# Two heads on the 128 partitions in place of one: softmax times V with 64 KB loads, 4 KB stores and products over the values of two heads

## The chip, the cores and the metric

One core of a Trainium2 chip runs the whole program. The metric is device time in microseconds (us), the median of several executions; smaller is better.

## The reference

```python
# scores [8, 12, 1024, 1024] f32, v [8, 12, 1024, 64] f32: 96 heads
scores_max = np.max(scores, axis=-1, keepdims=True)
attn = np.exp(scores - scores_max)
attn = attn / (np.sum(attn, axis=-1, keepdims=True) + 1e-8)
return np.matmul(attn, v).astype(np.float32)      # [8, 12, 1024, 64]
```

The scores are 4 MB per head, 403 MB in all, and each is used once. That is why the loads matter so much.

## The kernel before

One head at a time stands on the 128 partitions, with 8 query rows in each (`R = 8`). Its scores come as one 4 MB transfer, in which each partition receives one run of 32 KB. Four such tiles are in flight (`AHEAD = 4`), and the load of head n+4 is queued when head n has been read. ScalarE takes the exponential of two rows per partition and writes float16. TensorE transposes eight 128x128 blocks, VectorE copies them to SBUF, and TensorE multiplies them with the values and a column of ones, whose product is the sum of the row. VectorE divides, four rows at a time.

```python
    R = SQ // P          # 8
    M = D + 1            # 65
    EB = 2; G = 4; LAG = 2; NV = 3
    AHEAD = 4
    sc_bh = scores.rearrange("b h (p r) j -> (b h) p r j", p=P)
    # ... (cut: views of v and out, pools)
    s_pool = ctx.enter_context(tc.tile_pool(name="spool", bufs=AHEAD))
    # ... (cut)
    def finish(u):
        # ... (cut)
        for c in range(C):
            nc.tensor.matmul(out=psO[:, g, :], lhsT=pt[:, c * P : (c + 1) * P],
                             rhs=st["vones"][:, c, :], start=(c == 0), stop=(c == C - 1))
        if g == G - 1:
            # ... (cut: reciprocal of the sums)
            nc.vector.tensor_tensor(out=st["out_sb"][:, r - G + 1 : r + 1, :],
                in0=psO[:, :, 0:D], in1=recip[:].to_broadcast([P, G, D]), op=mybir.AluOpType.mult)
        if r == R - 1:
            queue(nc.sync.dma_start(out=out_bh[n], in_=st["out_sb"][:]))
    def load(n):
        v_sb = v_pool.tile([P, C, D], FP32, tag="v_sb", name="v_sb")
        queue(nc.sync.dma_start(out=v_sb[:], in_=v_bh[n]))
        s_nat = s_pool.tile([P, R, SK], FP32, tag="s_nat", name="s_nat")
        step = EB if n == BH - 1 else R          # the last head in four pieces
        for r in range(0, R, step):
            queue(nc.sync.dma_start(out=s_nat[:, r : r + step, :], in_=sc_bh[n, :, r : r + step, :]))
    # ... (cut)
        for r in range(R):
            if r % EB == 0:
                p_nat = p_pool.tile([P, EB, SK], FP16, tag="p_nat", name="p_nat")
                nc.scalar.activation(out=p_nat[:], in_=s_nat[:, r : r + EB, :], func=EXP)
            # ... (cut: eight transposes into psT, one copy to pt)
            if r == R - 1 and n + AHEAD < BH:
                load(n + AHEAD)
            # ... (cut: finish() two rows later)
```

All transfers are issued by one queue, in program order.

The softmax here doesn't subtract the row's maximum and nothing guards it: scores larger than these inputs give would overflow.

Of the kernel before, what the change touches and what calls it, by code (L numbers as in the profile page):

```python
# [1 line left out]

# [5 lines left out]

FP32 = mybir.dt.float32
FP16 = mybir.dt.float16  # L10
EXP = mybir.ActivationFunctionType.Exp


@with_exitstack
def kernel(
    ctx: ExitStack,
    tc: tile.TileContext,
    scores: bass.AP,
    v: bass.AP,
    out: bass.AP,  # L20
):
    nc = tc.nc
    P = 128

    B, H, SQ, SK = scores.shape
    Bv, Hv, SKv, D = v.shape
    assert (B, H, SK) == (Bv, Hv, SKv)
    BH = B * H
    assert SQ % P == 0 and SK % P == 0
    R = SQ // P  # L30
    C = SK // P
    M = D + 1
    EB = 2
    G = 4
    LAG = 2
    NV = 3
    AHEAD = 4



    sc_bh = scores.rearrange("b h (p r) j -> (b h) p r j", p=P)
    v_bh = v.rearrange("b h (p c) d -> (b h) p c d", p=P)
    out_bh = out.rearrange("b h (p r) d -> (b h) p r d", p=P)

    const_pool = ctx.enter_context(tc.tile_pool(name="const", bufs=1))
    s_pool = ctx.enter_context(tc.tile_pool(name="spool", bufs=AHEAD))
    p_pool = ctx.enter_context(tc.tile_pool(name="ppool", bufs=6))
    v_pool = ctx.enter_context(tc.tile_pool(name="vpool", bufs=AHEAD))
    pt_pool = ctx.enter_context(tc.tile_pool(name="ptpool", bufs=5))
    ob_pool = ctx.enter_context(tc.tile_pool(name="obpool", bufs=3))  # L50
    rc_pool = ctx.enter_context(tc.tile_pool(name="rcpool", bufs=4))
    psT_pool = ctx.enter_context(tc.tile_pool(name="psTp", bufs=5, space=bass.MemoryType.PSUM))
    psO_pool = ctx.enter_context(tc.tile_pool(name="psOp", bufs=3, space=bass.MemoryType.PSUM))

    ident32 = const_pool.tile([P, P], FP32, name="ident32")
    make_identity(nc, ident32)
    ident16 = const_pool.tile([P, P], FP16, name="ident16")
    nc.vector.tensor_copy(out=ident16[:], in_=ident32[:])  # L58


    vones_bufs = []
    for k in range(NV):
        vo = const_pool.tile([P, C, M], FP16, name=f"vones{k}")
        nc.vector.memset(vo[:, :, D : D + 1], 1.0)  # L64
        vones_bufs.append(vo)

    pending = []

    def finish(u):

        n, r, pt, st = u
        g = r % G
        if g == 0:
            st["psO"] = psO_pool.tile([P, G, M], FP32, tag="psO", name="psO")
        psO = st["psO"]
        for c in range(C):
            nc.tensor.matmul(  # L77
                out=psO[:, g, :],
                lhsT=pt[:, c * P : (c + 1) * P],
                rhs=st["vones"][:, c, :],  # L80
                start=(c == 0),
                stop=(c == C - 1),
            )
        if g == G - 1:
            if r == G - 1:
                st["out_sb"] = ob_pool.tile([P, R, D], FP32, tag="out_sb", name="out_sb")
            recip = rc_pool.tile([P, G, 1], FP32, tag="recip", name="recip")
            nc.vector.reciprocal(out=recip[:], in_=psO[:, :, D : D + 1])  # L88
            nc.vector.tensor_tensor(  # L89
                out=st["out_sb"][:, r - G + 1 : r + 1, :],  # L90
                in0=psO[:, :, 0:D],
                in1=recip[:].to_broadcast([P, G, D]),
                op=mybir.AluOpType.mult,
            )
        if r == R - 1:
            queue(nc.sync.dma_start(out=out_bh[n], in_=st["out_sb"][:]))  # L96

    queued = []

    def queue(dma):  # L100

        if queued:
            tc.add_manual_dep(
                dma.ins,
                queued[-1].ins.name,
                mybir.DependencyInfo(mybir.DependencyClass.NoSync, mybir.DependencyReason.DATA),
                reason="queue order",
            )
        queued.append(dma)

    loaded = {}

    def load(n):
        v_sb = v_pool.tile([P, C, D], FP32, tag="v_sb", name="v_sb")
        queue(nc.sync.dma_start(out=v_sb[:], in_=v_bh[n]))  # L115
        s_nat = s_pool.tile([P, R, SK], FP32, tag="s_nat", name="s_nat")
        step = EB if n == BH - 1 else R
        for r in range(0, R, step):
            queue(
                nc.sync.dma_start(out=s_nat[:, r : r + step, :], in_=sc_bh[n, :, r : r + step, :])  # L120
            )
        loaded[n] = (s_nat, v_sb)

    for n in range(min(AHEAD, BH)):
        load(n)

    for n in range(BH):
        s_nat, v_sb = loaded.pop(n)
        vones = vones_bufs[n % NV]
        nc.gpsimd.tensor_copy(out=vones[:, :, 0:D], in_=v_sb[:])  # L130
        st = dict(vones=vones)

        for r in range(R):
            if r % EB == 0:
                p_nat = p_pool.tile([P, EB, SK], FP16, tag="p_nat", name="p_nat")
                nc.scalar.activation(out=p_nat[:], in_=s_nat[:, r : r + EB, :], func=EXP)  # L136
            p_row = p_nat[:, r % EB, :].rearrange("p (q c) -> p c q", c=C)
            psT = psT_pool.tile([P, SK], FP16, tag="psT", name="psT")
            for c in range(C):
                nc.tensor.transpose(  # L140
                    out=psT[:, c * P : (c + 1) * P],
                    in_=p_row[:, c, :],
                    identity=ident16[:],
                )
            pt = pt_pool.tile([P, SK], FP16, tag="pt", name="pt")
            nc.vector.tensor_copy(out=pt[:], in_=psT[:])  # L146
            if r == R - 1 and n + AHEAD < BH:
                load(n + AHEAD)
            pending.append((n, r, pt, st))
            if len(pending) > LAG:  # L150
                finish(pending.pop(0))
    while pending:
        finish(pending.pop(0))


# [1 line left out]
_INS = ['scores', 'v']  # L157
_OUTS = [((8, 12, 1024, 64), 'float32')]


# [23 lines left out]
```

## Time and profile before

| | before |
|---|---|
| median of 3 executions | 1090.04 us (1089.73 to 1090.33) |
| span of the profiled one | 1088.4 us |
| DMA slices at 9 tenths | 39 of 40 |
| bytes moved | 454.77 MB, 418 GB/s on average |
| busiest compute engine | PE, 72% |
| head 93 landed / last scores landed / end | 1054.3 / 1077.1 / 1088.4 us |

### The profile page before, as it was taken

How to read it: one execution, taken by the hardware profiler on the slowest of the kernel's cores; microseconds unless marked ns; L12 is line 12 of the kernel's file. 1: busy time of each engine (PE TensorE's matmuls, PEld its weight loads, DVE VectorE, ACT ScalarE, POOL GpSimd, SP SyncE). 2: the span in 40 equal slices, each digit the busy share in tenths (PEclk: the TensorE clock that was granted, in tenths of full speed). 3: DMA queues.
4: the chain of work that ended last, by engine and by line, in shares of the span. 5: the costliest groups of instructions: out<-in, count | busy, mean ns of one | idle time of the engine just before them, and what ended most of it. 6: DMA issues, size and time to landing. Idle time of an engine off the chain costs nothing.

```text
span 1088.4 us, 27687 instructions
## 1 busy us (share of the span) xinstructions
PE 782.8 (72%) x12288; PEld 743.7 (68%) x12288; DVE 628.2 (58%) x1156; ACT 704.0 (65%) x385; POOL 60.1 (6%) x102
## 2 busy tenths in 40 slices
PE   3767777676777767677776767777676777767676
PEld 3667667676766767677676767677676767767676
DVE  2556556565555655556565655655565565556555
ACT  4667576666757666665766666575665757566675
POOL 0000000000000000000000000000000000000000
PEclk9888878778787877878888887878888787787888
DMA  9999999999999999999999999999999999999994
GB/s 396 423 430 425 423 423 427 427 426 428 427 422 423 424 431 427 422 426 424 431 425 429 425 426 424 425 429 428 424 423 430 424 426 427 428 420 428 426 398 160
DMA packets 42024, 454.77 MB, mean 418 GB/s; under 512 B 4656, under 2 KB 4656, under 8 KB 29232
## 3 DMA queue, kind: packets, MB, share of 16 engines
q1 hardware_dynamic: 41904, 453.00, 98.5%
q8 instruction: 96, 1.57, 0.6%
q14 instruction: 24, 0.20, 0.0%
HBM read 427.82 MB, written 25.17 MB: 416 GB/s over the span
## 4 chain that ended last, share of the span: by engine, by line
DMA 96%; DVE 1%; PE 1%; issue 0%; SPq 0%; ACT 0%; DVEq 0%; ACTq 0%
DMA out_dram<-out_sb 69%; DMA s_nat<-in_scores_dram 18%; DMA v_sb<-in_v_dram 9%; DVE out_sb L89 1%; PE psT L140 1%; PE psO L77 0%; SPq L120 0%; ACT p_nat L136 0%; DVE pt L146 0%; SPq L115 0%; DVE recip L88 0%; DVEq L89 0%; SPq L96 0%; ACTq L136 0%
## 5 line engine op out<-in xcount | busy, mean ns | idle before, releaser
L136 ACT ACTIVATE p_nat<-s_nat 128x2048 f16<-128x2048 f32 x384 | 702.8, 1901 | 375.8 <-DMA s_nat<-in_scores_dram 364.7
L140 PE MATMUL psT<-ident,p_nat 128*128 128x128 f16 x6144 | 621.6, 264 | 274.5 <-ACT p_nat L136 273.5
L140 PEld LDWEIGHTS <-p_nat 128*128 128x128 f16 x6144 | 524.9, 155 | 301.5 <-ACT p_nat L136 295.2
L146 DVE COPY pt<-psT 128x1024 f16<-128x1024 f16 x768 | 529.0, 691 | 307.2 <-PE psT L140 285.4
L77 PE MATMUL psO<-vones,pt 128*128 128x65 f16 x6144 | 343.0, 204 | 27.3 <-DVE pt L146 26.3
L77 PEld LDWEIGHTS <-pt 128*128 128x128 f16 x6144 | 295.4, 107 | 39.2 <-DVE pt L146 38.3
L89 DVE TENSOR_TENSOR out_sb<-psO,recip 128x256 f32<-128x256 f32 x192 | 73.6, 420 | 98.7 <-DMA out_dram<-out_sb 98.6
L130 POOL CAST vones<-v_sb 128x512 f16<-128x512 f32 x96 | 59.4, 619 | 1007.3 <-DMA v_sb<-in_v_dram 995.5
L88 DVE RECIPROCAL recip<-psO 128x4 f32<-128x4 f32 x192 | 34.1, 178 | 49.9 <-PE psO L77 49.9
L136 ACT ACT_TABLE_LOAD x1 | 1.3, 1283 | 0.7 <-PEq L168 0.7
L64 DVE MEMSET vones<- 128x8 f16 x3 | 0.1, 65 | 0.8 <-PEq L168 0.8
L58 DVE CAST ident<-ident 128x128 f16<-128x128 f32 x1 | 0.2, 227 | 0.4 <-POOL ident masks.py:199 0.4
masks.py:199 POOL TENSOR_SCALAR_AFFINE_SELECT ident<-ident 128x128 f32<-128x128 f32 x1 | 0.3, 294 | 0.1
masks.py:197 POOL MEMSET ident<- 128x128 f32 x1 | 0.2, 205 | 0.3 <-POOLq L168 0.3
L168 POOL MEMSET const-float32-0.0<- 128x1 f32 x1 | 0.1, 99 | 0.2 <-issue 0.2
L168 POOL MEMSET const-bfloat16-1.0<- 128x1 bf16 x1 | 0.1, 102 | 0.0
L168 POOL MEMSET const-uint8-127<- 128x1 uint8 x1 | 0.1, 102 | 0.0
L168 POOL MEMSET const-float32-1.0<- 128x1 f32 x1 | 0.1, 99 | 0.0
## 6 DMA issues: line engine op xcount, KB each, us to landing
s_nat<-in_scores_dram SPq DMA_DIRECT2D x95, 4096.0 KB, 32.5
v_sb<-in_v_dram SPq DMA_DIRECT2D x96, 256.0 KB, 23.5
out_dram<-out_sb SPq DMA_DIRECT2D x96, 256.0 KB, 32.4
s_nat<-in_scores_dram SPq DMA_DIRECT2D x4, 1024.0 KB, 23.8
```

What stands on the lines that cost most here:

```text
L58: nc.vector.tensor_copy(out=ident16[:], in_=ident32[:])
L64: nc.vector.memset(vo[:, :, D : D + 1], 1.0)
L77: nc.tensor.matmul(out=psO[:, g, :], lhsT=pt[:, c * P : (c + 1) * P], rhs=st["vones"][:, c, :], start=(c == 0), stop=(c == C - 1),)
L88: nc.vector.reciprocal(out=recip[:], in_=psO[:, :, D : D + 1])
L89: nc.vector.tensor_tensor(out=st["out_sb"][:, r - G + 1 : r + 1, :], in0=psO[:, :, 0:D], in1=recip[:].to_broadcast([P, G, D]), op=mybir.Al ...
L130: nc.gpsimd.tensor_copy(out=vones[:, :, 0:D], in_=v_sb[:])
L136: nc.scalar.activation(out=p_nat[:], in_=s_nat[:, r : r + EB, :], func=EXP)
L140: nc.tensor.transpose(out=psT[:, c * P : (c + 1) * P], in_=p_row[:, c, :], identity=ident16[:],)
L146: nc.vector.tensor_copy(out=pt[:], in_=psT[:])
L168: nc = _bacc.Bacc("TRN2", target_bir_lowering=False, num_devices=1)
```

## The change

The intent: let two heads share the partitions, 64 partitions each with 16 query rows, so that scores come as runs of 64 KB and the output leaves as runs of 4 KB. The partitions then belong to two heads, so a product takes the values of both heads at once (129 columns: 64 values, the ones, 64 values) and each half of the partitions keeps its own half. The tiles double, so two of them fit (`AHEAD = 2`).

```diff
-    R = SQ // P
-    M = D + 1
+    HALF = P // 2
+    NP = BH // 2
+    R = SQ // HALF          # 16
+    W = 2 * D + 1           # 129
-    AHEAD = 4
+    AHEAD = 2
-    sc_bh = scores.rearrange("b h (p r) j -> (b h) p r j", p=P)
+    sc = scores.rearrange("b h i j -> (b h i) j").rearrange("(k p r) j -> k p r j", p=P, r=R)
 ... (cut: v and out likewise; psT buffers 5 to 4, psO buffers 3 to 2)
-        step = EB if n == BH - 1 else R
-        for r in range(0, R, step):
+        cuts = [0, R]
+        if k == 0:
+            cuts = list(range(0, R + 1, 4))
+        if k == NP - 1:
+            cuts = list(range(0, R - 1, EB)) + [R - 1, R]
+        for a, b in zip(cuts, cuts[1:]):
+            queue(nc.sync.dma_start(out=s_nat[:, a:b, :], in_=sc[k, :, a:b, :]))
 ... (cut)
-                out=psO[:, g, :],
+                out=psO[:, g, 0:W],
 ... (cut)
-            nc.vector.tensor_tensor(... 128 partitions ...)
+            for h in range(2):
+                rows = slice(h * HALF, (h + 1) * HALF)
+                nc.vector.tensor_tensor(
+                    out=st["out_sb"][rows, r - G + 1 : r + 1, :],
+                    in0=psO[rows, :, h * (D + 1) : h * (D + 1) + D],
+                    in1=recip[rows].to_broadcast([HALF, G, D]),
 ... (cut)
-            if r == R - 1 and n + AHEAD < BH:
-                load(n + AHEAD)
+            if r == R - 1 and k + AHEAD < NP:
+                load(k + AHEAD)
```

The exponential of the very last two rows is also cut in two.

More of the change, by code (lines that the diff above doesn't have):

```diff
@@ L28 @@
     BH = B * H
-    assert SQ % P == 0 and SK % P == 0
-    R = SQ // P
+    HALF = P // 2
+    assert SQ % P == 0 and SK % P == 0 and BH % 2 == 0
+    NP = BH // 2
+    R = SQ // HALF
     C = SK // P
-    M = D + 1
+    W = 2 * D + 1
     EB = 2
@@ L36 @@
     NV = 3
-    AHEAD = 4
-    sc_bh = scores.rearrange("b h (p r) j -> (b h) p r j", p=P)
-    v_bh = v.rearrange("b h (p c) d -> (b h) p c d", p=P)
-    out_bh = out.rearrange("b h (p r) d -> (b h) p r d", p=P)
+    AHEAD = 2
+    sc = scores.rearrange("b h i j -> (b h i) j").rearrange("(k p r) j -> k p r j", p=P, r=R)
+    ov = out.rearrange("b h i d -> (b h i) d").rearrange("(k p r) d -> k p r d", p=P, r=R)
+    vv = v.rearrange("b h j d -> (b h) j d").rearrange("(k a) (p c) d -> k p a c d", a=2, p=P)
     const_pool = ctx.enter_context(tc.tile_pool(name="const", bufs=1))
@@ L51 @@
     rc_pool = ctx.enter_context(tc.tile_pool(name="rcpool", bufs=4))
-    psT_pool = ctx.enter_context(tc.tile_pool(name="psTp", bufs=5, space=bass.MemoryType.PSUM))
-    psO_pool = ctx.enter_context(tc.tile_pool(name="psOp", bufs=3, space=bass.MemoryType.PSUM))
+    psT_pool = ctx.enter_context(tc.tile_pool(name="psTp", bufs=4, space=bass.MemoryType.PSUM))
+    psO_pool = ctx.enter_context(tc.tile_pool(name="psOp", bufs=2, space=bass.MemoryType.PSUM))
     ident32 = const_pool.tile([P, P], FP32, name="ident32")
@@ L62 @@
     for k in range(NV):
-        vo = const_pool.tile([P, C, M], FP16, name=f"vones{k}")
+        vo = const_pool.tile([P, C, W], FP16, name=f"vones{k}")
         nc.vector.memset(vo[:, :, D : D + 1], 1.0)
@@ L67 @@
     pending = []
-    def finish(u):
-        n, r, pt, st = u
-        g = r % G
-        if g == 0:
-            st["psO"] = psO_pool.tile([P, G, M], FP32, tag="psO", name="psO")
-        psO = st["psO"]
-        for c in range(C):
-            nc.tensor.matmul(
-                out=psO[:, g, :],
-                lhsT=pt[:, c * P : (c + 1) * P],
-                rhs=st["vones"][:, c, :],
-                start=(c == 0),
-                stop=(c == C - 1),
-            )
-        if g == G - 1:
-            if r == G - 1:
-                st["out_sb"] = ob_pool.tile([P, R, D], FP32, tag="out_sb", name="out_sb")
-            recip = rc_pool.tile([P, G, 1], FP32, tag="recip", name="recip")
-            nc.vector.reciprocal(out=recip[:], in_=psO[:, :, D : D + 1])
-            nc.vector.tensor_tensor(
-                out=st["out_sb"][:, r - G + 1 : r + 1, :],
-                in0=psO[:, :, 0:D],
-                in1=recip[:].to_broadcast([P, G, D]),
-                op=mybir.AluOpType.mult,
-            )
-        if r == R - 1:
-            queue(nc.sync.dma_start(out=out_bh[n], in_=st["out_sb"][:]))
     queued = []
@@ L111, with load @@
     loaded = {}
-    def load(n):
-        v_sb = v_pool.tile([P, C, D], FP32, tag="v_sb", name="v_sb")
-        queue(nc.sync.dma_start(out=v_sb[:], in_=v_bh[n]))
+    def load(k):
+        v_sb = v_pool.tile([P, 2, C, D], FP32, tag="v_sb", name="v_sb")
+        queue(nc.sync.dma_start(out=v_sb[:], in_=vv[k]))
         s_nat = s_pool.tile([P, R, SK], FP32, tag="s_nat", name="s_nat")
-        step = EB if n == BH - 1 else R
-        for r in range(0, R, step):
-            queue(
-                nc.sync.dma_start(out=s_nat[:, r : r + step, :], in_=sc_bh[n, :, r : r + step, :])
-            )
-        loaded[n] = (s_nat, v_sb)
@@ L124 @@
-    for n in range(min(AHEAD, BH)):
-        load(n)
-    for n in range(BH):
-        s_nat, v_sb = loaded.pop(n)
-        vones = vones_bufs[n % NV]
-        nc.gpsimd.tensor_copy(out=vones[:, :, 0:D], in_=v_sb[:])
+        cuts = [0, R]
[5 more added lines that the diff above has]
+            queue(nc.sync.dma_start(out=s_nat[:, a:b, :], in_=sc[k, :, a:b, :]))
@@ new lines, in load, with finish @@
+        loaded[k] = (s_nat, v_sb)
+    def finish(u):
+        k, r, pt, st = u
+        g = r % G
+        if g == 0:
+            st["psO"] = psO_pool.tile([P, G, 256], FP32, tag="psO", name="psO")
+        psO = st["psO"]
+        for c in range(C):
+            nc.tensor.matmul(
+                out=psO[:, g, 0:W],
+                lhsT=pt[:, c * P : (c + 1) * P],
+                rhs=st["vones"][:, c, :],
+                start=(c == 0),
+                stop=(c == C - 1),
+            )
+        if g == G - 1:
+            if r == G - 1:
+                st["out_sb"] = ob_pool.tile([P, R, D], FP32, tag="out_sb", name="out_sb")
+            recip = rc_pool.tile([P, G, 1], FP32, tag="recip", name="recip")
+            nc.vector.reciprocal(out=recip[:], in_=psO[:, :, D : D + 1])
+            for h in range(2):
[4 more added lines that the diff above has]
+                    in1=recip[rows].to_broadcast([HALF, G, D]),
+                    op=mybir.AluOpType.mult,
+                )
+        if r == R - 1:
+            queue(nc.sync.dma_start(out=ov[k], in_=st["out_sb"][:]))
@@ L131 @@
+    for k in range(min(AHEAD, NP)):
+        load(k)
+    for k in range(NP):
+        s_nat, v_sb = loaded.pop(k)
+        vones = vones_bufs[k % NV]
+        for h in range(2):
+            nc.gpsimd.tensor_copy(
+                out=vones[:, :, h * (D + 1) : h * (D + 1) + D], in_=v_sb[:, h, :, :]
+            )
         st = dict(vones=vones)
@@ L135 @@
                 p_nat = p_pool.tile([P, EB, SK], FP16, tag="p_nat", name="p_nat")
-                nc.scalar.activation(out=p_nat[:], in_=s_nat[:, r : r + EB, :], func=EXP)
+                parts = [(0, 1), (1, 2)] if (k == NP - 1 and r == R - EB) else [(0, EB)]
+                for a, b in parts:
+                    nc.scalar.activation(
+                        out=p_nat[:, a:b, :], in_=s_nat[:, r + a : r + b, :], func=EXP
+                    )
             p_row = p_nat[:, r % EB, :].rearrange("p (q c) -> p c q", c=C)
@@ L146 @@
             nc.vector.tensor_copy(out=pt[:], in_=psT[:])
-            if r == R - 1 and n + AHEAD < BH:
-                load(n + AHEAD)
-            pending.append((n, r, pt, st))
+            if r == R - 1 and k + AHEAD < NP:
+                load(k + AHEAD)
+            pending.append((k, r, pt, st))
             if len(pending) > LAG:
```

## The prediction

> **What bounds the kernel now.** I read the page's slices and queue table first, then the chain, then the costliest groups, then the chain in order of time near the end, and last the single packets that the trace records. From the page (tenths of busy time per slice; GB/s moved; then the queue's share, and the shares of the chain):
>
> ```profile
> ACT  4667576666757666665766666575665757566675
> DMA  9999999999999999999999999999999999999994
> GB/s 396 423 430 425 423 423 427 427 426 428 427 422 423 424 431 427 422 426 424 431 425 429 425 426 424 425 429 428 424 423 430 424 426 427 428 420 428 426 398 160
> ...
> q1 hardware_dynamic: 41904, 453.00, 98.5%
> q8 instruction: 96, 1.57, 0.6%
> ...
> DMA 96%; DVE 1%; PE 1%; issue 0%; SPq 0%; ACT 0%; DVEq 0%; ACTq 0%
> ```
>
> The DMA engines are full in 39 of 40 slices at about 426 GB/s, and 96% of the chain is DMA. No compute engine passes 72%. The groups say the same: ScalarE's idle time before its exponentials is 364.7 us of waiting for scores.
>
> ```profile
> L136 ACT ACTIVATE p_nat<-s_nat 128x2048 f16<-128x2048 f32 x384 | 702.8, 1901 | 375.8 <-DMA s_nat<-in_scores_dram 364.7
> L146 DVE COPY pt<-psT 128x1024 f16<-128x1024 f16 x768 | 529.0, 691 | 307.2 <-PE psT L140 285.4
> L77 PE MATMUL psO<-vones,pt 128*128 128x65 f16 x6144 | 343.0, 204 | 27.3 <-DVE pt L146 26.3
> L89 DVE TENSOR_TENSOR out_sb<-psO,recip 128x256 f32<-128x256 f32 x192 | 73.6, 420 | 98.7 <-DMA out_dram<-out_sb 98.6
> ```
>
> So bytes per time decide until the last scores land; after that, compute decides. The chain in order of time (start us, us, what) shows that end:
>
> ```profile
> 1032.79 33.13 DMA s_nat<-in_scores_dram
> ...
> 1066.02 1.92 ACT p_nat L136
> ...
> 1067.98 2.87 PE psT L140 x24
> 1070.85 0.44 PE psO L77 x8
> 1071.29 0.85 PE psT L140 x8
> ...
> 1075.08 0.53 PE psT L140 x8
> 1075.61 0.26 PE psO L77 x8
> ...
> 1084.80 0.42 DVE out_sb L89
> ```
>
> Head 94 lands at 1065.9; its work and that of head 95 (which comes in four 1 MB pieces) take the remaining 22.4 us. PE begins slow (24 transposes in 2.87 us, 120 ns each) and is then at 0.53 us per eight transposes and 0.26 us per eight products, 0.79 us per block of 128 query rows (I call it a row).
>
> The packet records: a 32 KB scores packet takes 1216 ns (median), a 2 KB packet of v or of the output 84 ns, and the next packet on the engine starts about 3.5 ns before the old one is over. Two equations, 1212.5 = a + 32768/b and 80 = a + 2048/b, give b = 27.13 B/ns and a = 4.5 ns per packet. Only 4.5 ns are fixed: that is all that longer runs can save. The completion counts show something else: the 16 engines drift apart, 0.6 us between first and last on the first scores, 20 us at the end, since some engines also fetch the 16 KB instruction packets (about 1.05 us each). The last engine, which decides each landing, needs 11.2 us per head ((1065.91-13.53)/94), the first 10.99.
>
> **What the Trainium skill says.** (1) "DMA: Bandwidth & Descriptors", section "Where 436 GB/s comes from": 16 ports at 32 B and 850 MHz give 435.2 GB/s. The trace agrees: 16 x 27.13 = 434. The byte rate is at its ceiling. (2) Same page, "Why small descriptors are slow (HBM only)": about 3 cycles of overhead per packet, which matters at 256 B. My 4.5 ns is of that size, and our smallest data packet is 2 KB. (3) "TensorE: Matmul & The Clock Gate", "Back-to-back issue gap": the gap grows with the output columns N once N is over about 64. The trace has 33 ns for N=65 and 66 ns for N=128, so 129 columns should cost about 66 ns. (4) Same page, "HAM oscillation": idle gaps of a few us drop the clock to half. The trace shows it after a gap of 3.4 us (120 ns instead of 66 ns per transpose at 1067.98).
>
> **The change part by part.**
>
> 1. Scores. The bytes stay; the packets halve from 12,288 to 6,144 of 64 KB. Per pair of heads an engine moves 8 packets instead of 16: 8 x 4.5 = 36 ns saved.
> 2. Output. 4 KB runs instead of 2 KB: again 8 packets fewer per engine and pair, 36 ns. v keeps its 2 KB runs: nothing. Three transfers fewer per pair save three completion writes of about 6 ns each, 18 ns. Together 0.09 us per pair, on the path: over 47 pairs -4.2 us.
> 3. Products. 6144 of them stay 6144, since the pair count halves and the rows double; each goes from 65 to 129 columns, half of the output being thrown away. A row then costs 0.53 + 0.53 = 1.06 us of PE, a pair 16 x 1.06 = 17 us, plus about 1.7 us for a slow-clock start, of a 22.3 us period. Hidden, but no longer small.
> 4. Multiplies. Each of 192 becomes two on 64 partitions with 256 elements in each partition; I take the same 0.42 us for each, as the elements per partition are unchanged: +80 us of VectorE. Per four rows VectorE has 4 x 0.735 + 0.18 + 0.85 = 4.0 us against PE's 4.2. Hidden.
> 5. Buffers. Two 64 KB-per-partition tiles in place of four of 32 KB. The load of pair k+2 goes out when ScalarE has read pair k, 8 x 1.83 = 14.6 us after its landing; pair k+1 is due 22.3 us after it. About 6 us of queued work is left after the issue delay: no hole. The fast DMA engines, which now may lead by 20 us, can lead only by that margin and will idle, but they do not set the landings.
> 6. The end. This is where I expect the loss. Pair 46 lands whole, and with it the last 32 rows of work are open, twice what head 94 and 95 left. The last pair comes in nine pieces, but ScalarE and PE are still on pair 46. From that landing: 1.95 us to PE's first transpose (as at 1066.02), 32 rows x 1.06 = 33.8, slow start +1.7, then the finish as before from the last product's end (1084.5 to 1088.4, 3.9 us), +0.45 for the second multiply, +0.6 for the last output of 512 KB. Sum 42.4 us.
>
> When does pair 46 land? It holds heads 92 and 93. Head 93 landed at 1054.35; minus 4.2 (packets), minus 0.6 (one head's output fewer stands before it in the queue): 1049.5. End of the span 1049.5 + 42.4 = 1091.9. The measured time is 1.6 us over the span (1090.04 against 1088.4), so 1093.5 us. Of the +3.5 us, -4.8 come from the stream and +8.3 from a longer end, counted from the same last byte. The start, cut into four pieces, lets compute begin some 5 us earlier, but the DMA queue is full from the first us on, so it is worth nothing.
>
> **The rivals.**
>
> A. The longer runs raise the stream's rate. For it: the change aims there, and the mean is 426 GB/s under a 434 ceiling. Against: the fitted fixed cost gives 0.09 us per pair. If the last engine came up to the first one's pace (10.99 instead of 11.2 us per head, 20 us in all), the time would be near 1074. Instruction packets cause that difference, and their number hardly changes.
>
> B. The queue runs dry, since only two pairs fit. For it: ScalarE releases a tile after 14.6 us, and anything that holds ScalarE (full p_nat buffers behind a slow PE) eats the 6 us. A hole of 1 us per pair makes 1140. Against: six p_nat buffers hold 12 of 16 rows, and PE ends a pair some 20 us after its landing.
>
> C. PE becomes the bound. At 1.06 us per row plus the slow start it needs 19 to 20 of 22.3 us. If a row took 1.35 us, the period would be 22 to 23 us and the end 10 us longer: 1105 to 1130. Against: 66 ns per 128 columns is seen in the trace.
>
> D. PE does not drop its clock, since it idles less; and the end is partly covered, as ScalarE's part is. That takes 2 us off: about 1091.
>
> **Range and chances.** The stream's rate is well pinned (1 to 3 us of doubt); the end has a doubt of 4 us from rows that could be 0.1 us longer through VectorE's near-equal load. Range 1086 to 1103. Faster by over 2% (under 1068) would need more than rival A: 0.02. Slower by over 2% (over 1112) needs B or C: 0.05. Within 2%: 0.93.
>
> **What would show it.** Right: GB/s near 425 in all middle slices; scores packets of 64 KB at about 2424 ns; ScalarE idling on scores about once per pair; product groups at 66 ns apart; pair 46 landing near 1049 and some 42 us after it to the end, nearly all of it PE in the chain, while the GB/s of the last slice fall to almost nothing. Wrong: PE or ScalarE leading in the chain of the middle, DMA slices under 9 (rival B or C), or a landing of pair 46 more than 5 us from 1049 (rival A or a rate that depends on the address pitch of 64 KB, which no record here shows).

## More of the kernel before

The prediction shows the lines that carry this and says how to read them. Two views that it does not show are needed to compare with later. The first is a table of two long stretches (us from the start; then busy time of PE, its weight loads, VectorE, ScalarE and GpSimd, the granted clock, the DMA share and GB/s):

```profile
24.00:385.00 361.00, 262.69 (x4122) 249.12 (x4120) 210.65 (x388) 237.69 (x130) 20.41 (x33) 0.81 1.01 425
385.00:1050.00 665.00, 485.28 (x7597) 461.17 (x7596) 388.59 (x712) 435.09 (x239) 36.50 (x59) 0.80 1.01 426
```

The rate in the last column is the same in both stretches. The second is what the issuing queue waits for (line, what it waits for: total us, times, longest us):

```profile
SPq L115 <- DMA s_nat<-in_scores_dram: 803.6, 89, 10.4
```

Line 115 issues the values of the next head, and line 120 its scores right after. The queue's one large wait is for an older scores transfer to land. ScalarE's release of a tile is not in that line, and at line 120 the queue waits for it 13.3 us in all: it is early enough.

## The result, and the profile after

| | before | after |
|---|---|---|
| median | 1089.88 us (1089.63 to 1090.33, 4 runs) | 1101.16 us (1100.47 to 1104.37, 4 runs) |
| span of the profiled run | 1088.4 | 1102.6 |
| head 93, or pair 46, landed | 1054.3 | 1061.9 |
| last scores landed | 1077.1 | 1085.0 |
| from there to the end | 11.3 | 17.6 |

The ratio is 1.0109, with a 95% interval of 1.0088 to 1.0129. A ratio here is the mean time of one kernel's fast runs over the mean of the other's of the same rounds, so it is not quite the ratio of the medians. Executions over 1.5% slower than the fastest of the same kernel are left out of the means. The kernel is 1% slower, inside the predicted range, 7.7 us above the predicted time. The profiled run, 1104.37 us, is the slowest of its four; the other three have spans of 1098.7 to 1099.8 us. What its trace says of the stream therefore overstates the median run by up to about 3 us.

From the page of the changed kernel, the rate in 40 slices, the data queue (packets, MB, share) and the shares of the chain:

```profile
GB/s 417 429 418 406 442 429 428 420 431 440 415 435 418 436 429 406 423 435 422 413 422 422 420 430 432 398 442 405 415 414 417 429 410 403 413 412 429 420 380 92
...
q1 hardware_dynamic: 28464, 452.99, 97.8%
...
DMA 66%; ACT 22%; issue 7%; PE 3%; DVE 0%; ACTq 0%; SPq 0%; DVEq 0%
```

The packets fell from 41904 to 28464 for the same bytes. Yet the rate is not steadier: in the second half many slices lie between 398 and 417. And the chain, 96% DMA before, is now 66% DMA, 22% ScalarE and 7% issue: ScalarE stands between one load and the next. The same two stretches as before make it plain:

```profile
24.00:385.00 361.00, 277.18 (x3973) 266.96 (x3972) 224.22 (x435) 227.14 (x126) 20.18 (x34) 0.87 1.01 429
385.00:1050.00 665.00, 526.68 (x7520) 508.36 (x7519) 422.77 (x822) 427.69 (x237) 34.44 (x58) 0.88 1.01 419
```

Up to 385 us the changed kernel moves 429 GB/s, *more* than before's 425. After that it moves 419, less than before's 426. The DMA share in the column before the last is 1.01 in both: the engines count as busy, but get less done. The packet records agree: after 385 us fewer than 15 of the 16 engines have a packet open in about 0.5% of the time. The rate is not the loss itself, though: what an engine that runs ahead moves early counts in it, while nothing waits for it. The time lost is read from the landings. Per pair of heads and for the last of the 16 DMA engines, which decides each landing, the completion counts give 22.29 us over pairs 2 to 17 and 22.72 us from pair 18 on. Over 29 pairs the difference is 12.4 us.

The groups (busy us, mean ns, idle time and its main releaser) answer to those of the prediction:

```profile
L145 ACT ACTIVATE p_nat<-s_nat 128x2048 f16<-128x2048 f32 x385 | 697.8, 1895 | 391.2 <-DMA s_nat<-in_scores_dram 391.2
...
L106 PE MATMUL psO<-vones,pt 128*128 128x129 f16 x6144 | 513.6, 229 | 4.9 <-DVE pt L157 1.1
...
L120 DVE TENSOR_TENSOR out_sb<-psO,recip 64x256 f32<-64x256 f32 x384 | 162.2, 422 | 9.1
```

Compute behaves as predicted: the multiplies on 64 partitions take 422 ns each, as those on 128 did (420), and the wide products make PE busier without making it the bound. ScalarE still idles 391.2 us waiting for scores.

What did turn up is in the queue's waits and in the timeline of the middle (start us, length us, engine, what, and the idle time before it):

```profile
SPq L95 <- ACT p_nat L145: 653.0, 46, 14.6
```

```profile
515.01 14.54 ACT L145 ACTIVATE p_nat<-s_nat 128x2048 f16<-128x2048 f32 x8 [7.57 <-DMA s_nat<-in_scores_dram]
...
529.57 0.33 SPq L95 DMA_DIRECT2D s_nat<-in_scores_dram  x1
...
537.62 3.71 ACT L145 ACTIVATE p_nat<-s_nat 128x2048 f16<-128x2048 f32 x2 [8.07 <-DMA s_nat<-in_scores_dram]
```

A pair lands at 515.0; ScalarE reads it for 14.54 us; in the moment it is done, at 529.57, the next load goes out; and the pair that was still in flight lands at 537.6, 8.05 us later. So when a load is issued, the last DMA engine has 8 us of scores left in its queue. I call this time from the issue to the next landing **the margin**; over the run it lies between 7.0 and 9.0 us. A DMA engine that is ahead of the last by the margin has nothing left.

Are there such engines? Each of the 16 engines counts its own share of a transfer as done, and the transfer has landed with the sixteenth count. Before, the time from the first count to the sixteenth, which I call **the drift**, grows from 0.6 to 20.3 us, step by step. After, it grows to 8.5 us by pair 17 and then stays between 7 and 10 us: the very time from which the rate falls.

And how do they lose time? In single packets. A 64 KB scores packet takes 2421 ns in the median. The share of packets that take over 8% more rises from 1.9% (24 to 385 us) to 11.5% (385 to 1045 us); these take 2977 ns on average; four in five lie within 4 us of the issue of a scores load (one in three would by chance), and around some issues 16 of them are open at once, so all 16 engines have them. With eight packets per engine and pair, 8 x (0.115 - 0.019) x 0.56 us = 0.43 us per pair, which is the whole step from 22.29 to 22.72. Before, the two shares are 1.5% and 0.8%.

The end of the chain in order of time (start us, us, what), from that landing on (x24 and x8 count the instructions in a step):

```profile
1061.97 1.92 ACT p_nat L145
1063.93 2.89 PE psT L151 x24
1066.82 0.87 PE psO L106 x8
...
1072.18 0.50 PE psT L151 x8
...
1078.48 0.47 PE psO L106 x8
```

From 2 us after the landing of pair 46 until 1094.0 us PE works without a break: after a slow start of a few us at 0.50 us per eight transposes and 0.47 us per eight products, 0.97 us per row where the prediction had 1.06. The products of 129 columns start 59 ns apart, not 66. The end comes 40.7 us after that landing (1061.86 to 1102.6) against 42.4 predicted.

### The profile page after: what moved, and what is told of

Its sections match the earlier page's. It is cut to its first block, busy times and chain, and to the rows that moved or that the text cites. A ratio compares the mean times of both kernels' runs of the same rounds, so it can differ in the third digit from the quotient of the medians.

```text
span 1102.6 us, 27224 instructions
## 1 busy us (share of the span) xinstructions
PE 857.7 (78%) x12288; PEld 827.2 (75%) x12288; DVE 692.5 (63%) x1348; ACT 699.1 (63%) x386; POOL 57.7 (5%) x102
## 3 DMA queue, kind: packets, MB, share of 16 engines
q1 hardware_dynamic: 28464, 452.99, 97.8%
q8 instruction: 96, 1.57, 0.6%
## 4 chain that ended last, share of the span: by engine, by line
DMA 66%; ACT 22%; issue 7%; PE 3%; DVE 0%; ACTq 0%; SPq 0%; DVEq 0%
DMA s_nat<-in_scores_dram 66%; ACT p_nat L145 22%; PE psT L151 2%; PE psO L106 1%; ACTq L145 0%; DVE pt L157 0%; SPq L95 0%; DVE out_sb L120 0%; DVEq L190 0%; SPq L87 0%; DVE recip L117 0%
## 5 line engine op out<-in xcount | busy, mean ns | idle before, releaser
L145 ACT ACTIVATE p_nat<-s_nat 128x2048 f16<-128x2048 f32 x385 | 697.8, 1895 | 391.2 <-DMA s_nat<-in_scores_dram 391.2
L151 PE MATMUL psT<-ident,p_nat 128*128 128x128 f16 x6144 | 559.6, 244 | 235.1 <-ACT p_nat L145 234.9
L157 DVE COPY pt<-psT 128x1024 f16<-128x1024 f16 x768 | 508.4, 689 | 359.6 <-PE psT L151 355.0
L151 PEld LDWEIGHTS <-p_nat 128*128 128x128 f16 x6144 | 490.4, 151 | 250.8 <-ACT p_nat L145 246.2
L106 PE MATMUL psO<-vones,pt 128*128 128x129 f16 x6144 | 513.6, 229 | 4.9 <-DVE pt L157 1.1
L106 PEld LDWEIGHTS <-pt 128*128 128x128 f16 x6144 | 415.7, 103 | 19.6 <-DVE pt L157 13.3
L120 DVE TENSOR_TENSOR out_sb<-psO,recip 64x256 f32<-64x256 f32 x384 | 162.2, 422 | 9.1
L136 POOL CAST vones<-v_sb 128x512 f16<-128x512 f32 x96 | 57.0, 624 | 1007.4 <-DMA v_sb<-in_v_dram 986.0
```

The costliest lines, as they stand in the source:

```text
L106: nc.tensor.matmul(out=psO[:, g, 0:W], lhsT=pt[:, c * P : (c + 1) * P], rhs=st["vones"][:, c, :], start=(c == 0), stop=(c == C - 1),)
L120: nc.vector.tensor_tensor(out=st["out_sb"][rows, r - G + 1 : r + 1, :], in0=psO[rows, :, h * (D + 1) : h * (D + 1) + D], in1=recip[rows].t ...
L136: nc.gpsimd.tensor_copy(out=vones[:, :, h * (D + 1) : h * (D + 1) + D], in_=v_sb[:, h, :, :])
L145: nc.scalar.activation(out=p_nat[:, a:b, :], in_=s_nat[:, r + a : r + b, :], func=EXP)
L151: nc.tensor.transpose(out=psT[:, c * P : (c + 1) * P], in_=p_row[:, c, :], identity=ident16[:],)
L157: nc.vector.tensor_copy(out=pt[:], in_=psT[:])
```

## The experiments

Two theories for the lost stream. **L, late release:** two large tiles leave a margin of only 8 us; as soon as the drift between the DMA engines reaches it, the queues run nearly dry at each issue, and the stream loses time. **P, packets:** 64 KB packets, or the 64 KB pitch between partitions, are slower in themselves. A third, **H:** the heavier work of PE slows the transfers. The expectations below use these letters. Ratios are against the kernel before in the same rounds; unless said otherwise the result is correct.

**e1: each scores load in two transfers of eight rows.** Packets of 32 KB, in place of 64 KB.

```diff
-        cuts = [0, R]
+        cuts = [0, R // 2, R]
```

> The changed kernel, but each pair's scores come in two transfers of eight rows, so packets are 32 KB again; both are still issued only when the whole tile has been read. Theory L (the queue is too short: a tile is released 14.6 us after its landing, so the early engines catch up with the issue, and from then on the last engine is slowed too, about 0.45 us per pair): stays at 1099 to 1104 us, drift between the engines stops near 8 us as in the changed kernel. Theory P (64 KB packets themselves, at instruction fetches): 1090 to 1094 us, since the last engine would be back at 22.3 us per pair.

Measured: 1091.33 us (1090.15 to 1092.27), ratio 1.0015 (1.000 to 1.003). The loss is nearly gone, which looks like P. But the run was a flawed control: the first half lands first, so ScalarE starts earlier and also ends earlier. The queue's wait for ScalarE shows it:

```profile
SPq L95 <- ACT p_nat L145: 336.3, 46, 7.4
```

It is 7.4 us at most where the change had 14.6. So e1 changed packet size and margin together (the margin is now about 22.3 - 7.4 = 15 us). It does not separate these two; e3 and e5 do. It does speak against the pitch, which is still 64 KB here.

**e5: the same two transfers, in swapped order.** Rows 8 to 15 come first, so ScalarE must wait for the second transfer as it waited for the one before. Packets are 32 KB, and the release is late again.

```diff
+        pieces = list(zip(cuts, cuts[1:]))
+        if 0 < k < NP - 1:
+            pieces = [(R // 2, R), (0, R // 2)]
-        for a, b in zip(cuts, cuts[1:]):
+        for a, b in pieces:
```

> The control that the split run lacked: split in two, ScalarE could start on the first half 10 us early and so released the tile 7.3 us after the landing; that run too had an early release. Here the two 32 KB-packet transfers come in swapped order (rows 8 to 15 first), so ScalarE, which goes from row 0, has to wait for the second one, and the tile is released 14.6 us after the landing, as in the changed kernel. Theory L (late release, short queue): 1097 to 1105 us, drift stops near 8 us, scores packets stretched in the later part. Theory P (64 KB packets): 1090 to 1094 us.

Measured: 1105.04 us (1103.41 to 1105.53), ratio 1.0136 (1.0119 to 1.0153). The waits of its queue and the two stretches:

```profile
SPq L98 <- ACT p_nat L148: 655.8, 46, 14.6
```

```profile
24.00:385.00 361.00, 275.98 (x3964) 265.79 (x3963) 223.15 (x434) 225.88 (x125) 20.16 (x34) 0.87 1.01 426
385.00:1050.00 665.00, 525.10 (x7505) 506.91 (x7503) 422.38 (x820) 426.96 (x236) 34.38 (x58) 0.87 1.01 419
```

The whole loss is back with 32 KB packets: 426, then 419 GB/s. The drift stops at 8 to 9 us, the stretched packets rise from 1.0% to 7.5%. P falls: e5 has the small packets and the loss, e1 the same packets and pitch without it. The first stretch also shows what the packet size is worth: 426 against 429.

**e3: 64 KB packets, early release.** ScalarE does every second exponential only, so it frees a tile after half the time. The result is wrong.

```diff
-            if r % EB == 0:
+            if r % EB == 0 and (r % (2 * EB) == 0 or k == NP - 1):
```

> Wrong result on purpose: the changed kernel with 64 KB packets, but ScalarE makes exponentials of only two of every four rows (the other two reuse them), so it is done with a tile in half the time, 7.3 us after landing, and the next load is issued 7 us earlier. All PE and VectorE work stays. L: the stream is back at 22.3 us per pair, pair 46 lands near 1050, end unchanged at 40 to 41 us: 1090 to 1094 us. P: stays at 1099 to 1104 us.

Measured: 1093.50 us (1093.19 to 1094.45), ratio 1.0037 (1.0022 to 1.0052). With the changed kernel's packets and a margin of 15 us, pair 46 lands at 1051.4 us, 10.5 earlier than in the changed kernel's trace. Three stretches of it:

```profile
24.00:385.00 361.00, 277.18 (x3974) 269.55 (x3972) 224.35 (x436) 117.09 (x64) 20.13 (x34) 0.87 1.01 429
385.00:720.00 335.00, 266.79 (x3841) 259.54 (x3839) 216.39 (x421) 109.81 (x61) 17.75 (x30) 0.88 1.01 428
720.00:1050.00 330.00, 264.35 (x3810) 257.10 (x3808) 214.03 (x418) 104.38 (x58) 16.57 (x28) 0.88 1.00 423
```

The high rate now lasts until about 720 us, where the drift comes to 13 to 15 us (the margin of this kernel is 14.4 to 16 us in its trace). Then the rate falls here too, and the share of stretched packets rises from 1.0% to 5.3%. The fall is put off about in proportion to the margin. L is right so far.

**e4 and e11: the kernel before with two and with three tiles.** Nothing of the change but fewer tiles, at 32 KB packets. The margin is 11.15 - 7.4 = 3.8 us with two and 14.9 us with three; with the four of before the same sum gives 26 us. (With several loads in flight I count to the landing of the last of them.) But there the queue issues a load only when an older transfer has landed, as its wait at line 115 showed, and the trace has 21.5 us in the median.

```diff
-    AHEAD = 4
+    AHEAD = 2      # e4;  3 in e11
```

> The kernel before with two score tiles instead of four: 32 KB packets, the next load is issued 7.4 us after a landing, in a period of 11.2 us, so the margin is about 3 us. L: the drift stops near 3 us and the last engine is slowed for nearly the whole run, so clearly slower: 1100 to 1125 us. P: unchanged, 1089 to 1092 us.

> Dose test on the kernel before: three score tiles, so the next load is issued with about 14 us of work left instead of 3 (two tiles) or 26 (four). L: the drift grows undisturbed to 12 to 15 us, near 2/3 of the run, and only then do packets stretch: 1090 to 1096 us, between the 1089.7 of four tiles and the 1116 of two. If only a queue that runs dry mattered, not the drift: 1089 to 1090.

Measured: with two tiles 1103.33, 1114.72 and 1118.31 us (a fourth, 1121.2, was slow), ratio 1.0261 (1.0234 to 1.0287). The profiled run is the first and fastest of these; the others lost 11 to 15 us more, for which there is no trace. With three 1091.17 us (1090.80 to 1091.29), ratio 1.0012 (0.9999 to 1.0026). The stretches, first of e4, then of e11:

```profile
24.00:385.00 361.00, 261.43 (x4078) 248.53 (x4075) 204.85 (x382) 234.21 (x128) 19.77 (x32) 0.81 1.00 418
385.00:1050.00 665.00, 481.90 (x7487) 457.90 (x7484) 376.91 (x704) 428.97 (x235) 36.43 (x59) 0.80 1.01 418
```

```profile
385.00:720.00 335.00, 245.07 (x3830) 233.05 (x3828) 192.94 (x360) 218.16 (x121) 18.64 (x31) 0.80 1.01 426
720.00:1050.00 330.00, 239.99 (x3738) 228.21 (x3739) 188.21 (x350) 215.22 (x119) 18.02 (x30) 0.80 1.01 421
```

With two tiles the rate is 418 from the start, and the drift never passes 2 to 3.5 us. With three it is 426 until the drift reaches 13.2 us at 718 us, then 421. So the change's layout, packets and products are not needed for the loss. A short margin alone makes it. The readings of six kernels fit one rule: the drift stops where it meets the margin, and from there the last engine needs longer. The margin is worked out as the time for the scores still queued (11.15 us per head, 22.3 per pair) less the time that ScalarE takes to read a tile or half of it (7.4 or 14.6 us); of the changed kernel and of before it was read from the trace. The last column is the time that the last engine needs, in us per pair of heads, over pairs 2 to 17, 18 to 31 and 32 to 46:

| kernel | margin, us | where the drift stops, us | rate before and after that | last engine, us per pair |
|---|---|---|---|---|
| e4, two 32 KB tiles | 3.8 | 2 to 3.5 | 418 throughout | 22.69, 22.66, 22.73 |
| changed | 8.0 | 7 to 10 | 429, 419 | 22.29, 22.49, 22.94 |
| e5, swapped | about 8 | 8 to 9 | 426, 419 | 22.38, 22.53, 22.90 |
| e3, early release | about 15 | 14 to 17 | 428, 423 | 22.29, 22.27, 22.46 |
| e11, three 32 KB tiles | 14.9 | 13 to 15 | 426, 421 | 22.42, 22.35, 22.56 |
| before, four 32 KB tiles | 21.5 | not reached (20.3 at the end) | 426 throughout | 22.42, 22.37, 22.43 |

With a margin of 15 us the last engine loses 0.2 us per pair in the last third; with 8 us it loses about 0.2 in the middle and 0.5 to 0.65 in the last third. That the loss still grows while the drift stands still, the rule does not explain.

**e7: products and multiplies as light as before.** 65 columns and one multiply on 128 partitions; the second head of each pair comes out wrong. This tests H.

```diff
-                out=psO[:, g, 0:W],
+                out=psO[:, g, 0 : D + 1],
-                rhs=st["vones"][:, c, :],
+                rhs=st["vones"][:, c, 0 : D + 1],
-            for h in range(2):
-                rows = slice(h * HALF, (h + 1) * HALF)
+            for h in range(1):
+                rows = slice(0, P)
```

> Wrong result on purpose: the changed kernel with products of 65 columns (only the first head's values) and one multiply on 128 partitions, so PE and VectorE do per row what they did before. L and T: the stream is unchanged, the end becomes ScalarE's (32 rows at 0.915 us and about 5 us more, 35 us instead of 40.7): 1094 to 1098 us. Rival H (the heavier PE and VectorE slow the transfers): 1085 to 1090 us.

Measured: 1096.94 us (1094.42 to 1099.82), ratio 1.0068 (1.0048 to 1.0087), as expected. PE's busy time in the late stretch fell from 526.68 to 445.06 us, below before's 485.28, yet the rate stays low:

```profile
385.00:1050.00 665.00, 445.06 (x7610) 426.08 (x7609) 372.73 (x712) 430.56 (x237) 34.45 (x58) 0.81 1.00 421
```

The last engine needs 22.50 us per pair over pairs 18 to 31, as in the changed kernel (22.49). H falls as the cause of the loss. The gain of 4.2 us in the medians is no more than the end gives: 35.9 us from pair 46's landing in place of 40.7, with rows that are shorter by the 64 columns. The two profiled runs differ by another 5 us in that landing (1056.8 against 1061.9), but they are the fastest of e7 and the slowest of the changed kernel.

**e12: where the drift comes from.** One of eight products per row remains, so the program has 13,826 PE instructions in place of 24,578. The result is wrong.

```diff
-        for c in range(C):
+        for c in range(1):
 ...
-                stop=(c == C - 1),
+                stop=True,
```

> Wrong result on purpose: the changed kernel with one product of the eight per row, so TensorE has 13,826 instructions instead of 24,578. If the instruction packets cause the drift, it grows at 0.56 of its rate (11 us at the end of an unlimited run instead of 20): the 8 us limit is met near pair 33 instead of 18, the last engine needs about 22.15 us per pair until then, and pair 46 lands near 1045; the end is ScalarE's (about 35 us): 1080 to 1086 us. If the drift has another cause: it stops near 8 us by pair 18 as before, pair 46 lands near 1058, 1093 to 1097 us.

Measured: 1082.10 us (1081.88 to 1082.45), ratio 0.993 (0.9915 to 0.9945). Its queue of instruction packets (packets, MB, share), where the kernel before has 96:

```profile
q8 instruction: 54, 0.88, 0.3%
```

The drift came to 8.6 us only at pair 30, where the changed kernel had 8.5 at pair 17. The ratio of the two, 17/30 = 0.57, is close to that of the packets, 54/96 = 0.56. The steps say the same: until it stops, the drift rises by 1.2 to 1.6 us once in eight fetches, in the changed kernel at pairs 5, 9, 13 and 17, and here at 8, 15, 22 and 30; in e7, with lighter products but as many fetches, they stand at 5, 9, 13 and 17 again. So the fetches of instructions, which the engines do not share evenly, are what pulls some of them behind the others. Pair 46 lands at 1042.8 us, 19 us before the changed kernel's. This run also took most of the products from PE; since e7 halved their columns with little effect on the rate, I put the gain to the fetches, but the two are not fully apart.

**e2, e8, e10: the release in halves.** If L is right, the layout can be kept and the margin restored: four tiles of half a pair (8 rows, 32 KB runs), each released by its own half. e2 does this; e8 also takes pair 46 in pieces of four rows, to shorten the end; e10 also keeps TensorE's instructions in the order of the program.

```diff
-    s_pool = ctx.enter_context(tc.tile_pool(name="spool", bufs=AHEAD))
+    s_pool = ctx.enter_context(tc.tile_pool(name="spool", bufs=2 * AHEAD))
 ... (cut: load(k, half) fills one tile of R // 2 rows)
-            if r == R - 1 and k + AHEAD < NP:
-                load(k + AHEAD)
+            if r % HR == HR - 1 and k + AHEAD < NP:
+                load(k + AHEAD, r // HR)
 # e8 and e10 also:
+        if k == 0 or k == NP - 2:
             cuts = list(range(0, HR + 1, 4))
 # e10 also: a dependence from every transpose and product to the one before it
+            mm = nc.tensor.matmul(...)
+            pe(mm, mm)
```

> The changed kernel with four score tiles of half a pair instead of two of a whole one: 32 KB packets, and a tile is released 7.3 us after ScalarE starts on it. Both L and P expect the last engine at 22.3 us per pair and a drift that grows to about 15 us or more; the end also shortens, as half of pair 46 can be worked on before the other half lands: 1083 to 1089 us. If neither L nor P holds (for instance the heavier PE slows the transfers), it stays over 1095.

> Both remedies together: half-pair tiles (early release) and pair 46 in pieces of four rows. Stream as in the half-tile run (last scores near 1076.5), then one or two rows of work and the last output: end 8 to 9 us later, 1085 to 1088 us, the first version under the kernel before by 2 to 4 us.

> Half-pair tiles, pair 46 in pieces of four rows, and TensorE's order fixed. Stream as in the half-tile runs (last scores at 1077), end about 8 us later: 1085 to 1088 us, under the kernel before (1089.7) by 0.2 to 0.4%. If the end is not cured: 1090 or more.

Measured: e2 1090.49 us (1089.91 to 1091.08), ratio 1.0008 (0.9993 to 1.0023); e8 1091.62 us (1090.63 to 1091.97), ratio 1.0015 (1.0002 to 1.0029); e10 1087.52 us (1087.16 to 1087.75), ratio 0.9979 (0.9966 to 0.9991). The stream is healed in all three (drift up to 19.5 us, free to grow; pair 46 at 1052.9 to 1053.3). e10 in the late stretch:

```profile
385.00:1050.00 665.00, 526.23 (x7644) 518.09 (x7642) 431.42 (x838) 436.47 (x239) 34.46 (x58) 0.88 1.01 425
```

This is 425 with PE as busy as in the changed kernel (526), which speaks once more against H. But e2 and e8 missed their expectations by a few us, and the miss is in the end: 12.8 and 14.2 us from the last scores where e10 has 9.8. The chain of e8 shows why:

```profile
1075.86 0.70 DVE pt L168
1076.61 1.24 PE psO L113 x16
1077.85 0.51 PE psT L162 x8
1078.39 0.70 DVE pt L168
1079.14 1.26 PE psO L113 x16
```

TensorE was given sixteen products in a row, then the transposes of one row, and then waits for VectorE's copy of that row: the two engines take turns. The order of TensorE's instructions had changed with the pieces. With the order fixed, e10 is the one version with a correct result that beats both kernels: by 2.2 us before, under the 2% that count as faster, but with an interval that leaves 1 out, and by 13.6 us the change.

**e6 and e9: only the end of the changed kernel.** Pair 46 in four pieces, the tiles as in the change; e9 with TensorE's order fixed.

```diff
+        if k == NP - 2:
+            cuts = list(range(0, R + 1, 4))
```

> The changed kernel with pair 46 also loaded in pieces (four of four rows), so that ScalarE and PE follow the transfer at 1.2 us a row instead of starting with 32 open rows. The stream stays as it is. Theory T (the end is 8 us too long because 32 rows are open when pair 46 lands): 1090 to 1095 us, 6 to 10 us faster than the changed kernel, from the last scores to the end 8 to 11 us instead of about 16. If the end were bound otherwise: no change.

> The run with pair 46 in pieces lost part of its gain because the instruction order of TensorE changed at the end: sixteen products in a row, then transposes that wait for VectorE. Here the order of TensorE is fixed to the program's (eight transposes, eight products). Theory T: from the last scores to the end about 8 us instead of 14 (pieces, free order) and 17.6 (changed kernel); with the stream of the changed kernel (last scores at 1081 to 1085 us): 1089 to 1095 us.

Measured: e6 1098.39 us (1095.60 to 1101.09), ratio 1.008 (1.0059 to 1.0101), a miss, with 15.2 us from the last scores to the end and the same pattern of sixteen products, one row of transposes and a copy; the figure of 14 us that the expectation of e9 gives for it is too small. e9 1093.39 us (1092.26 to 1095.55), ratio 1.0036 (1.0022 to 1.0049), within its expected time, with an end of 11.9 us where I had thought of 8. So the order costs a few us in the end. The rest of e9's gain lies before: pair 46 landed at 1055.9 us in e9 and 1057.3 in e6, where the changed kernel's trace, its slowest run, has 1061.9. With a margin of 8 us the stream varies by some us from run to run. The order is not part of the change's own loss: the changed kernel's chain shows transposes and products of single rows in turn.

## Why the prediction was right or wrong

The time lay in the range, and "within 2%" held. The sum behind it was half right, and that the range still held the time is partly luck: it allowed 1 to 3 us for the stream, which was off by 9 to 12.

1. Packets, right as long as the drift is small. The saving of 0.09 us per pair gives 22.30 us; measured 22.29 over pairs 2 to 17, where before has 22.42. A 64 KB packet takes 2421 ns (2424 predicted). In the fit, 84 less 3.5 is 80.5, not 80; the fixed cost is then 5.0 ns in place of 4.5, which changes nothing.
2. Output runs: a 4 KB packet takes 159 ns in the median; they are part of the same 22.29.
3. Products: hidden, as said, and cheaper than said (59 ns each, not 66; 0.97 us per row, not 1.06).
4. Multiplies: 422 ns on half the partitions (420 predicted), hidden.
5. Buffers: **this is the step that failed.** It said "no hole", that the fast engines "can lead only by that margin and will idle", and that "they do not set the landings". The margin was computed well (about 6 us after the issue delay; the trace has 8.05 from the issue), and the lead did stop there. But in the packet records they hardly idle, and once their lead had stopped, the last engine became slower too: from then on packets on all engines stretch around many issues, 0.43 us per pair and 12.4 us over 29 pairs in the profiled run. Pair 46 landed at 1061.9 there, not at 1049.5; the prediction had named a landing more than 5 us off as a sign of being wrong. The median of the four spans, 1099.35, is 3.3 us shorter; if that lies in the stream, the median run lost about 9 us. Only the profiled run has a trace, so this split is an inference. The stream term was to be -4.8 us against before and came out at +7.5 us in the profiled run (1061.9 against 1054.3), and at about +4 in the median one.
6. The end, right: 40.7 us from pair 46's landing (42.4 predicted). Together: 9.1 us more stream less 1.7 us of end give +7.4 us on the predicted time, against +7.7 measured. (The rest: a measured time is 1.8 us over its span in these runs, not 1.6.)

Of the rivals, B had the right sign without its size: ScalarE does stand in the chain (22%, behind the 66% of DMA), where the prediction had named its leading there as a mark of B, but at 0.43 us per pair, not whole microseconds, and through slower packets rather than a hole in the last engine's queue. A and C did not occur: the first stretch gained 1% in rate, and PE never set the pace before the end. D's 2 us in the end came about nearly in size (1.7), but from shorter rows; the slow start of PE was still there.

What stays open: why packets on *every* engine stretch once the leaders run out of work, and why the loss still grows afterwards. It is not the packet size (e5), not the change's PE load (e7, e10), and not the number of fetches as such (before has as many without it). The records show where the packets stretch, not what holds them. Nor is it shown which engines fetch; and e12 leaves open which part of its gain is fetches and which is PE.

## What to carry to other kernels

When a queue of transfers is the bound, count the work left in it at the moment the next load is issued, and compare it with how far the DMA engines drift apart, not with zero: 8 us of queue looked safe, and cost 1% because the engines drift by up to 20. A large tile is released only when all of it has been read; smaller tiles in the same memory, or a load cut in two so that reading starts earlier, give the margin back. And when transfers are cut into pieces at the end, look at the order of TensorE's instructions again, since it may have changed with them.

## What the Trainium skill lacked or had wrong

- "Trainium Kernel Development and Optimization", section "Best Practices", advises to double-buffer so that DMA and compute overlap. It does not say how much work must be queued. Here two buffers were too few: 1101.2 us (changed) and 1103.3 to 1118.3 us (e4) with two, 1091.2 with three, 1089.7 with four. A margin of 8 us cost 0.43 us per pair of heads; 21.5 us cost nothing.
- "Runtime: NRT & Kernel Launch", section "Instruction fetch mechanics", says that instructions are refilled in blocks of 16 KiB, and that crossing a block is mostly hidden. The block size agrees (96 packets, 1.57 MB). For the data transfers the cost is not hidden when the DMA engines are the bound: each fetch takes about 1.05 us on an engine that also carries data, and the engines drift apart by 20 us; with 54 packets in place of 96 (and less PE work) the changed kernel took 1082.1 in place of 1101.2 us. No page names this cost for data transfers.
- No page gives a measured time for a single data packet of 32 or 64 KB: 1216 and 2421 ns here, that is, 5 to 8 ns per packet and the rest bytes. Longer runs save next to nothing: 426 GB/s with 32 KB (e5), 429 with 64 KB, before the drift meets the margin.
- No page says what happens to the others when some DMA engines run out of queued work: packets on all 16 stretch, 11.5% of them by a quarter (2977 against 2421 ns).
